# The last quarter of an MLP's second product in a seven-product form, and its LayerNorm on three engines

## The chip, the cores and the metric

The kernel runs on one core of a Trainium2 chip. A core has five engines that run side by side, each through its own queue in order: TensorE (PE) multiplies matrices into PSUM, VectorE (DVE), ScalarE (ACT) and GpSimd (POOL) work elementwise, and SyncE (SP) issues DMAs; ScalarE and GpSimd issue DMAs too. The metric is the time of one execution in microseconds on the device.

## What is computed

A decoder layer for 512 tokens of width 1024: LayerNorm, a token mixer, LayerNorm, an MLP with squared ReLU and hidden width 4096, LayerNorm. What this change touches is the end:

```python
h = layer_norm(DEEPNORM_ALPHA * h + mix, ln1_g[l], ln1_b[l])
ff = jnp.square(jax.nn.relu(h @ w_ff1[l])) @ w_ff2[l]
h = layer_norm(DEEPNORM_ALPHA * h + ff, ln2_g[l], ln2_b[l])
```

All is float32. Each float32 operand is split into a high part (rounded to a reduced float32) and a low part, the rest, and a product of two operands is three matmuls: high by high, high by low, low by high. The split of a weight tile is a copy on ScalarE (`hi`) and a subtraction on VectorE (`lo`), lines 180 and 181.

## The kernel before

**Stages.** The token mixer ends in line 1016; from there on the kernel works on `h1T`, the normalised tokens with channels on the partitions, and on `res`, four tiles of 128 tokens x 1024, which already hold alpha times the normalised tokens and to which the MLP is added. The hidden width is worked through in four quarters (`FC = 4`, line 323, loop in line 1135). A quarter has 1024 hidden channels in eight tiles of 128. Its first product (`gemm_fm`, line 221) makes the hidden tiles in blocks of 2 or 4 (`F1`, line 324); `ev_h` (line 1142) evicts them from PSUM with a ReLU and squares them.

**The second product, quarters one to three** (`win_f2`, line 1100). It is a scheme of Strassen's kind (Winograd's variant), seven products of half-sized blocks for eight. The 512 tokens are halved (token tiles 0, 1 and 2, 3), the output columns are halved (j = 0 and 1, 512 each), and the hidden tiles are taken in pairs. `win_sums` (line 1064) makes sums of weight blocks (T1, T2, T3; T4 in line 1122), `win_hid` (line 1082) sums of hidden blocks. `WIN` (line 327) lists the products: a name for the weight block, which half of the hidden pairs (`hf`), and a phase `ph` from 0 to 6. An entry is 2 pairs x 2 token tiles x 3 = 12 matmuls with 512 columns; 14 entries make 168 matmuls. Phases 0, 3 and 6 add onto one pair of PSUM banks, 2 and 5 onto another, 1 and 4 have their own. After the second half of a phase the bank, as it stands, is copied to an SBUF tile `ev` by ScalarE (line 1128) and added to one or two blocks of `res` by accumulating DMAs from GpSimd's queue (line 1130). A bank that is added to further can be written again only when its copy is done.

**The second product, last quarter** (line 1177 on). It is the plain form: `gemm_tm` (line 246) for token tiles 0 and 1, then 2, and then tile 3 written out, its last 512 columns in two halves of 256 (line 1185). VectorE adds the result from PSUM to `res` (`ev_res`, line 991).

**LN2** (`ln2`, line 1038) for a token tile: statistics and their aggregate on VectorE, a power of -0.5 on GpSimd (line 1047), then for each column half two passes on VectorE, subtract the mean and multiply by g (line 1050), multiply by the reciprocal deviation and add b (line 1051), and a DMA to the output. g and b are loaded to all partitions by `bcast_row` (line 98).

**What sets the order.** Weights come through one list `stream`; `pump` (line 157) issues the loads on SP two entries ahead and the splits one or two ahead. In quarters one to three the weights of the second product are loaded whole by `win_load` (line 1055) on GpSimd's queue, eight tiles of 512 KB, for the next quarter after the tenth entry (line 1131). `HOMES` (line 325) says into which buffers an entry's split goes: `w` has two of each, `r` uses the three buffers of the raw weights, `a` a pool of 24. Small work is spread between matmuls as generators (`spawn`, `tick`, `finish`, lines 196 to 216). The pool B has 22 buffers (line 58); `h1T` holds 16 of them until the last first product, a22 (line 1094) one per hidden pair until phase 4, and `relu` and `ev` use the rest. On top of this the framework plans the order of each engine's instructions and the buffers with a timeline of its own (`schedule_with_timeline_sim`, line 1243): an instruction whose operands or buffer are ready by that timeline can go ahead of one written earlier. On the chip each engine then keeps the planned order. `tc.issue_after` adds an instruction's place behind another on the same engine.

Of the kernel before, what the change touches and what calls it, by code (L numbers as in the profile page):

```python
# [10 lines left out]
F32 = mybir.dt.float32  # L11
# [41 lines left out]
def tile_hybrid_block(ctx: ExitStack, tc: tile.TileContext, I, out, dbg=None):  # L53
# [267 lines left out]


    FC = 4
    F1 = [((0, 4), (4, 2), (6, 2))] + [tuple((b, 2) for b in range(0, 8, 2))] * 2 + [((0, 4), (4, 4))]
    HOMES = "wwrawarawawawa"
    HOME = {"w": ("whi", "wlo"), "r": ("wraw", "wraw"), "a": ("xh", "xl")}
    WIN = (("11", 0, 0), ("21", 0, 1), ("11", 1, 0), ("21", 1, 1), ("T1", 0, 2), ("T1", 1, 2), ("T2", 0, 3), ("T2", 1, 3),
           ("T4", 0, 4), ("T4", 1, 4), ("22", 0, 5), ("22", 1, 5), ("T3", 0, 6), ("T3", 1, 6))
    fb = 0
    for ci in range(FC):  # L330
        nb = 8
        for b, w in F1[ci]:
            PL["f1", ci, b] = plan("w_ff1", (fb + b) * P, w * P, res=(ci == 0 and b == 0), per=8 // w)
        if ci < FC - 1:
            PL["f2", ci] = []
            for n, (op, hf, _) in enumerate(WIN):
                PL["f2", ci].append(len(stream))
                stream.append({"src": lambda q=(ci, op, hf): WQ[q], "nk": 2, "n": T, "res": False,
                               "ahead": 2, "home": HOMES[n]})
        else:  # L340
            plan_zip("f2last", [("w_ff2", 0, fb, True), ("w_ff2", T, fb, True)])
        fb += nb


# [693 lines left out]
    def ln2(tt, bst=None):  # L1038
        mv = S([P, 2], F32, "mv")
        r = res[tt]  # L1040
        if bst is None:
            bst = S([P, 2, 6], F32, "bst")
            for j in range(2):
                nc.vector.bn_stats(bst[:, j, :], r[:, j * T:(j + 1) * T])
        nc.vector.bn_aggr(mv, bst)
        vts(mv[:, 1:2], mv[:, 1:2], LN_EPS, None, op0=ALU.add)
        gtt(mv[:, 1:2], mv[:, 1:2], mhalf[:, 0:1], op=ALU.pow)
        for j in range(2):
            c = slice(j * T, (j + 1) * T)
            stt(r[:, c], r[:, c], mv[:, 0:1], bg[:, c], op0=ALU.subtract, op1=ALU.mult)  # L1050
            stt(r[:, c], r[:, c], mv[:, 1:2], bb[:, c], op0=ALU.mult, op1=ALU.add)
            nc.sync.dma_start(out[tt * P:(tt + 1) * P, c], r[:, c])
        yield

    def win_load(ci):
# [43 lines left out]

    def win_f2(ci, hid):  # L1100
        bank = {}
        for n, (op, hf, ph) in enumerate(WIN):
            i = PL["f2", ci][n]
            pump(i)
            hi, lo = stream[i]["w"]
            for pp in range(2):
                for t in range(2):
                    key = ({3: 0, 6: 0, 5: 2}.get(ph, ph), t)
                    opens = key not in bank
                    if opens:  # L1110
                        bank[key] = (PX if key[0] < 2 else MM)()
                    o, c = bank[key], slice(t * P, (t + 1) * P)
                    while ph not in hid[2 * hf + pp]:
                        tick(4)
                    xh, xl = hid[2 * hf + pp][ph]
                    mm(o, xh[:, c], hi[:, pp], start=opens, stop=False, skip_group_check=True)  # L1116
                    mm(o, xh[:, c], lo[:, pp], start=False, stop=False, skip_group_check=True)  # L1117
                    mm(o, xl[:, c], hi[:, pp], start=False, stop=hf == 1 and pp == 1, skip_group_check=True)  # L1118
                tick(4)
            if n in (5, 6):  # L1120
                t2, q21 = WT.pop((ci, n - 5))
                vtt(t2, t2, q21, op=ALU.subtract)
                WQ[ci, "T4", n - 5] = t2
            if hf == 1:
                for t in range(2):
                    o = bank[{3: 0, 6: 0, 5: 2}.get(ph, ph), t]
                    e = B([P, T], F32, "ev")
                    st["ev"] = act(e, o, AF.Copy, scale=-1.0 if ph == 4 else 1.0)  # L1128
                    for tt, j in (((0, 0),), ((0, 0),), ((2, 1),), ((0, 1),), ((2, 0),), ((0, 1),), ((2, 0), (2, 1)))[ph]:
                        nc.gpsimd.dma_start(res[tt + t][:, j * T:(j + 1) * T], e, accum_op=ALU.add)  # L1130
            if n == 9 and ci + 1 < FC - 1:
                win_load(ci + 1)

    WQ, WT = {}, {}
    for ci in range(FC):
        nb = 8
        hid = []
        win = ci < FC - 1
        if ci == 0:
            win_load(0)  # L1140

        def ev_h(a, ps):
            r = B([P, T], F32, "relu")
            act(r, ps, AF.Relu)  # L1144
            if win:
                if a % 2 == 0:
                    hid.append({"R": A([P, 2, T], F32, "hr")})
                ops = hid[-1]
                R = ops["R"]
                act(R[:, a % 2, :], r, AF.Square)  # L1150
                if a % 2:
                    h1 = A([P, 2, 2, 256], F32R, "h1p")
                    split(R[:, :, :256], h1[:, 0], h1[:, 1])
                    ops[0], ops[1] = [(h1[:, 0, i], h1[:, 1, i]) for i in range(2)]
                    spawn(win_hid(R, ops))
                return
            hh = A([P, 2, T], F32R, "hid0")
            act(hh[:, 0, :], r, AF.Square)
            gtt(r, r, r, op=ALU.mult)
            vtt(hh[:, 1, :], r, f(hh[:, 0, :]), op=ALU.subtract)  # L1160
            hid.append(hh)
        for b, w in F1[ci]:
            if ci == 0 and b == 0:
                gemm_fm(PL["f1", ci, b], h1T, T, ev_h, toks=slice(256, T), accs=accs)
                t_r1 = spawn(residual1())
            else:
                gemm_fm(PL["f1", ci, b], h1T, w * P, ev_h, width=2)
            if win and b == 0:
                t_ws = spawn(win_sums(ci))
        if ci == 0:  # L1170
            finish(t_r1)
        if win:
            finish(t_ws)
            for hf in range(2):
                WT[ci, hf] = (WQ[ci, "T2", hf], WQ[ci, "21", hf])
            win_f2(ci, hid)
        else:
            bg, bb = bcast_row("ln2_g"), bcast_row("ln2_b")
            gemm_tm(PL["f2last"], hid, T, ev_res, tts=(0, 1))
            spawn(ln2(0))  # L1180
            spawn(ln2(1))
            gemm_tm(PL["f2last"], hid, T, ev_res, tts=(2,))
            spawn(ln2(2))
            tt, r, bst = 3, res[3], S([P, 4, 6], F32, "bst4")
            for c0, n in ((0, T), (T, 256), (T + 256, 256)):
                acc = MM()[:, :n]
                ws = slice(c0 % T, c0 % T + n)
                for k in range(nb):
                    hi, lo = weights(PL["f2last"][c0 // T], k)
                    xh, xl = hid[k][:, 0, tt * P:], hid[k][:, 1, tt * P:]  # L1190
                    mm(acc, xh, hi[:, ws], start=k == 0, stop=False)
                    mm(acc, xh, lo[:, ws], start=False, stop=False)
                    mm(acc, xl, hi[:, ws], start=False, stop=k == nb - 1)
                    tick(None)
                vtt(r[:, c0:c0 + n], acc, r[:, c0:c0 + n], op=ALU.add)
                for j in range(c0 // 256, (c0 + n) // 256):
                    nc.vector.bn_stats(bst[:, j, :], r[:, j * 256:(j + 1) * 256])
            finish(spawn(ln2(3, bst)))


# [46 lines left out]
```

## Time and profile before

| | us |
|---|---|
| median of 3 runs (lowest, highest) | 903.61 (903.56, 903.88) |
| the profiled execution | 902.75 |
| its span, first to last instruction | 901.0 |
| MLP, first quarter's second product starts | 605.1 |
| second quarter's | 686.7 |
| last quarter's first MLP product ends, its second starts | 849.9 |

A profile row names the start and length in us, the engine, the source line and the operation, what is written <- what is read, and in brackets how long the engine sat idle before it and what it waited for. PE is the matmul, PEld the load of its stationary operand. A matmul's length contains its latency; two that follow each other start closer than that. Rows "xN" hold N instructions in a row.

### The profile page before, as it was taken

The page shows a single profiled execution, that of the slowest core. Times are in us where ns is not written, and L with a number is a line of the kernel's source. Part 1 is how long each engine was busy: PE and PEld are TensorE (multiplying, and loading weights), DVE is VectorE, ACT ScalarE, POOL GpSimd, SP SyncE. Part 2 cuts the span into 40 slices and gives each one's busy share as a digit, 9 for nine tenths or more (in the row PEclk, how much of TensorE's full clock was granted, in tenths as well). Part 3 has the DMA queues.
Part 4 walks back from the last instruction along what each step waited for, and adds up shares of the span by engine and source line. Part 5 has one row for each costly group of instructions (what it writes and reads, how often), then busy time and mean ns, then how long its engine had stood idle before and what let it go on. Part 6 is the DMA issues. An engine that isn't in the chain of part 4 may idle for free.

```text
span 901.0 us, 11740 instructions
## 1 busy us (share of the span) xinstructions
PE 883.8 (98%) x4508; PEld 751.3 (83%) x4508; DVE 553.4 (61%) x905; ACT 412.7 (46%) x701; POOL 170.1 (19%) x192
## 2 busy tenths in 40 slices
PE   6999999999999999999999999999999999999996
PEld 5988888888888888888888888988888888888886
DVE  7835855575635244657756797997557646723576
ACT  6455443444434333435645423366357546643410
POOL 1003442442511010000000002104400520141201
PEclk9999999999999999999999999999999999999999
DMA  7413313212212332212207618005950990494312
GB/s 244 121 47 94 91 51 94 71 47 71 76 38 92 88 105 70 72 41 66 94 24 258 210 47 303 2 0 138 301 121 25 265 247 25 107 213 104 126 69 83
DMA packets 61159, 97.80 MB, mean 109 GB/s; under 512 B 7552, under 2 KB 27392, under 8 KB 61104
## 3 DMA queue, kind: packets, MB, share of 16 engines
q1 hardware_dynamic: 48816, 68.23, 23.9%
q0 software_dynamic: 10368, 25.17, 11.6%
q10 hardware_dynamic: 1920, 3.66, 1.2%
q8 instruction: 35, 0.57, 0.3%
q14 instruction: 20, 0.16, 0.1%
HBM read 82.36 MB, written 2.10 MB: 94 GB/s over the span
## 4 chain that ended last, share of the span: by engine, by line
PE 97%; ACT 1%; POOL 1%; DVE 1%; DMA 1%; issue 0%; SPq 0%; DVEq 0%
PE mm L231 16%; PE mm L233 15%; PE mm L232 15%; PE mm L264 7%; PE mm L266 7%; PE mm L265 7%; PE px L1116 2%; PE px L1118 2%; PE px L1117 2%; PE mm L1116 2%; PE mm L1118 2%; PE mm L1117 2%; PE px L679 2%; PE px L836 1%; PE px L366 1%; PE px L264 1%
## 5 line engine op out<-in xcount | busy, mean ns | idle before, releaser
L181 DVE TENSOR_TENSOR wlo<-wraw,whi 128x1024 fp32r<-128x1024 f32 (+1 forms) x104 | 117.7, 1133 | 169.6 <-ACT whi L180 162.2
L231 PE MATMUL mm<-h,whi 128*128 128x512 f32 x416 | 162.6, 392 | 0.4 <-ACT gt L923 0.4
L232 PE MATMUL mm<-h,whi 128*128 128x512 f32 x416 | 162.3, 390 | 0.0
L180 ACT ACTIVATE whi<-wraw 128x1024 fp32r<-128x1024 f32 (+1 forms) x104 | 100.3, 964 | 134.1 <-PE mm L232 82.4
L233 PE MATMUL mm<-h,wlo 128*128 128x512 f32 x416 | 154.4, 390 | 0.0
L231 PEld LDWEIGHTS mm<-h,whi 128*128 128x128 f32 x416 | 78.1, 188 | 16.3 <-ACT gt L923 0.6
L233 PEld LDWEIGHTS mm<-h,wlo 128*128 128x128 f32 x416 | 77.9, 188 | 16.4 <-DVE wlo L181 0.3
L232 PEld LDWEIGHTS mm<-h,whi 128*128 128x128 f32 x416 | 78.1, 188 | 15.7
L1130 POOL DMA_DIRECT2D res<-ev x48 | 42.2, 1042 | 188.9 <-ACT ev L1128 151.5
L265 PE MATMUL mm<-wlo,h 128*128 128x512 f32 x128 | 50.3, 393 | 0.0
L266 PE MATMUL mm<-whi,h 128*128 128x512 f32 x128 | 50.1, 392 | 0.0
L264 PE MATMUL mm<-whi,h 128*128 128x512 f32 x128 | 49.7, 403 | 0.0
L351 POOL TENSOR_TENSOR mv<-mv,mhalf 128x1 f32<-128x1 f32 x4 | 4.6, 1155 | 211.5 <-DVE mv L350 211.5
L180 ACT ACTIVATE xh<-wraw 128x1024 fp32r<-128x1024 f32 (+1 forms) x28 | 27.3, 986 | 34.8 <-PE mm L266 16.1
L618 POOL TENSOR_TENSOR rp<-rp 128x256 f32<-128x256 f32 x32 | 31.5, 984 | 60.8 <-ACT E L623 44.0
L1144 ACT ACTIVATE relu<-mm 128x512 f32<-128x512 f32 x32 | 18.8, 596 | 50.7 <-PE mm L233 50.6
L625 DVE TENSOR_TENSOR M<-E,qk 128x512 f32<-128x512 f32 x32 | 27.3, 854 | 16.5 <-ACT E L623 16.5
L181 DVE TENSOR_TENSOR xl<-wraw,xh 128x1024 fp32r<-128x1024 f32 (+1 forms) x28 | 31.1, 1126 | 8.0 <-ACT xh L180 8.0
L623 ACT ACTIVATE E<-rp 128x512 f32<-128x512 f32 x32 | 20.4, 638 | 26.9 <-POOL rp L619 26.9
L619 POOL TENSOR_TENSOR rp<-rp 128x256 f32<-128x256 f32 x32 | 27.6, 862 | 10.3 <-ACT q L648 8.1
L266 PEld LDWEIGHTS mm<-whi,h 128*128 128x128 f32 x128 | 24.1, 188 | 5.0
L265 PEld LDWEIGHTS mm<-wlo,h 128*128 128x128 f32 x128 | 24.1, 188 | 4.3
(369 smaller groups left out, 2196.1 us busy)
## 6 DMA issues: line engine op xcount, KB each, us to landing
wraw<-in_w_in_dram SPq DMA_DIRECT2D x40, 512.0 KB, 3.5
wraw<-in_w_ff_dram SPq DMA_DIRECT2D x40, 512.0 KB, 4.5
wq<-in_w_ff_dram POOLq DMA_DIRECT2D x24, 512.0 KB, 8.8
res<-ev POOLq DMA_DIRECT2D x48, 256.0 KB, 6.6
wraw<-in_w_o_gla_dram SPq DMA_DIRECT2D x8, 512.0 KB, 3.7
wraw<-in_w_o_mla_dram SPq DMA_DIRECT2D x8, 512.0 KB, 3.2
wraw<-in_w_out_dram SPq DMA_DIRECT2D x8, 512.0 KB, 4.0
wraw<-in_w_in_dram SPq DMA_DIRECT2D x8, 360.0 KB, 5.1
```

The source lines that it names most:

```text
L180: st["ins"] = act(hi[:, :nk, :n], raw[:, :nk, :n], AF.Copy)
L181: vtt(lo[:, :nk, :n], raw[:, :nk, :n], f(hi[:, :nk, :n]), op=ALU.subtract)
L231: mm(o, hi[:, c], xh, start=first, stop=False)
L232: mm(o, hi[:, c], xl, start=False, stop=False)
L233: mm(o, lo[:, c], xh, start=False, stop=last)
L264: mm(o, xh, hi[:, :n], start=opens, stop=False, skip_group_check=share)
L265: mm(o, xh, lo[:, :n], start=False, stop=False, skip_group_check=share)
L266: mm(o, xl, hi[:, :n], start=False, stop=last, skip_group_check=share)
L1116: mm(o, xh[:, c], hi[:, pp], start=opens, stop=False, skip_group_check=True)
L1117: mm(o, xh[:, c], lo[:, pp], start=False, stop=False, skip_group_check=True)
L1118: mm(o, xl[:, c], hi[:, pp], start=False, stop=hf == 1 and pp == 1, skip_group_check=True)
L1130: nc.gpsimd.dma_start(res[tt + t][:, j * T:(j + 1) * T], e, accum_op=ALU.add)
```

## The change

The last quarter's second product takes the seven-product form too. Its weights are loaded by `win_load` like those of the others, its hidden tiles go through the same sums and splits, and its first product uses blocks of two. In `WIN` the entries of the weight block 22 (phase 5) and of T4 (phase 4) change places, for all quarters.

In the last quarter the first eight entries run as in the others, with eight copies and eight accumulating DMAs. The last six are regrouped by token tile: 22 for tile 0, 22 for tile 1, then T3 and T4 for tile 2, then T3 and T4 for tile 3, the T4 of tile 3 in two halves of 256 columns. These are added to `res` (or subtracted) by VectorE straight from PSUM, without a copy and a DMA.

LN2 of tiles 0 to 2 goes over three engines: the normalisation in one pass on ScalarE, the multiplication by g on VectorE (tile 0 first half and tile 2 second half: on GpSimd), the addition of b on GpSimd. The second half of tile 2 is put behind the power of tile 3 in GpSimd's order. Tile 3 keeps its four passes on VectorE, the two that need no power first.

```diff
-    F1 = [((0, 4), (4, 2), (6, 2))] + [tuple((b, 2) for b in range(0, 8, 2))] * 2 + [((0, 4), (4, 4))]
+    F1 = [((0, 4), (4, 2), (6, 2))] + [tuple((b, 2) for b in range(0, 8, 2))] * 3
...
     WIN = (("11", 0, 0), ("21", 0, 1), ("11", 1, 0), ("21", 1, 1), ("T1", 0, 2), ("T1", 1, 2), ("T2", 0, 3), ("T2", 1, 3),
-           ("T4", 0, 4), ("T4", 1, 4), ("22", 0, 5), ("22", 1, 5), ("T3", 0, 6), ("T3", 1, 6))
+           ("22", 0, 5), ("22", 1, 5), ("T4", 0, 4), ("T4", 1, 4), ("T3", 0, 6), ("T3", 1, 6))
...
+                           "ahead": 2, "home": "r" if ci == FC - 1 and n == 12 else HOMES[n]})
...
-        gtt(mv[:, 1:2], mv[:, 1:2], mhalf[:, 0:1], op=ALU.pow)
+        rstd = gtt(mv[:, 1:2], mv[:, 1:2], mhalf[:, 0:1], op=ALU.pow)
+        if tt == 3:
+            st["pow3"] = rstd
+        else:
+            nmr = S([P, 1], F32, "nmr")
+            stt(nmr, mv[:, 0:1], -1.0, mv[:, 1:2], op0=ALU.mult, op1=ALU.mult)
         for j in range(2):
             c = slice(j * T, (j + 1) * T)
-            stt(r[:, c], r[:, c], mv[:, 0:1], bg[:, c], op0=ALU.subtract, op1=ALU.mult)
-            stt(r[:, c], r[:, c], mv[:, 1:2], bb[:, c], op0=ALU.mult, op1=ALU.add)
-            nc.sync.dma_start(out[tt * P:(tt + 1) * P, c], r[:, c])
+            if tt < 3:
+                act(r[:, c], r[:, c], AF.Identity, scale=mv[:, 1:2], bias=nmr)
+                with ExitStack() as gates:
+                    if (tt, j) == (2, 1):
+                        while "pow3" not in st:
+                            yield
+                        gates.enter_context(tc.issue_after(st["pow3"].ins))
+                    (gtt if (tt, j) in ((0, 0), (2, 1)) else vtt)(r[:, c], r[:, c], gb[0][:, c], op=ALU.mult)
+                    gtt(r[:, c], r[:, c], gb[1][:, c], op=ALU.add)
+                nc.sync.dma_start(out[tt * P:(tt + 1) * P, c], r[:, c])
+            else:
+                stt(r[:, c], r[:, c], mv[:, 0:1], gb[0][:, c], op0=ALU.subtract, op1=ALU.mult)
+        if tt == 3:
+            yield
+            for j in range(2):
+                c = slice(j * T, (j + 1) * T)
+                stt(r[:, c], r[:, c], mv[:, 1:2], gb[1][:, c], op0=ALU.mult, op1=ALU.add)
+                nc.sync.dma_start(out[tt * P:(tt + 1) * P, c], r[:, c])
...
+        for n, (op, hf, ph) in enumerate(WIN[:8] if end else WIN):
+            pump(PL["f2", ci][n])
...
+            if end and n == 6:
+                gb.extend([bcast_row("ln2_g"), bcast_row("ln2_b")])
...
-            if n == 9 and ci + 1 < FC - 1:
+            if n == 9 and not end:
                 win_load(ci + 1)
...
+        pump(PL["f2", ci][13])
...
+        for t in range(2):
+            o = tile_product((8, 9), t)
+            vtt(res[t][:, T:], res[t][:, T:], o, op=ALU.add)
+            spawn(ln2(t))
+        bst = S([P, 4, 6], F32, "bst4")
+        for t in range(2):
+            r = res[2 + t]
+            o = tile_product((12, 13), t)
+            for j in (1, 0):
+                vtt(r[:, j * T:(j + 1) * T], r[:, j * T:(j + 1) * T], o, op=ALU.add)
+            if t == 0:
+                o = tile_product((10, 11), t)
+                vtt(r[:, :T], r[:, :T], o, op=ALU.subtract)
+                t_ln2 = spawn(ln2(2))
+                continue
+            for j in range(2):
+                nc.vector.bn_stats(bst[:, 2 + j, :], r[:, T + j * 256:T + (j + 1) * 256])
+            for j in range(2):
+                c = slice(j * 256, (j + 1) * 256)
+                o = tile_product((10, 11), t, j * 256, 256, PX()[:, :256])
+                vtt(r[:, c], r[:, c], o, op=ALU.subtract)
+                nc.vector.bn_stats(bst[:, j, :], r[:, c])
+        finish(spawn(ln2(3, bst)), t_ln2)
```

`product` (new, inside `win_f2`) is the old body of the loop, the three matmuls of one hidden pair and token tile; `tile_product` calls it for two entries, that is 12 matmuls, of one token tile. The plain form of the last quarter, its `plan_zip` and the squarings on GpSimd (line 1159) go.

More of the change, by code (lines that the diff above doesn't have):

```diff
@@ L1137, in tile_hybrid_block @@
         hid = []
-        win = ci < FC - 1
         if ci == 0:
@@ L1171, in tile_hybrid_block @@
             finish(t_r1)
[L1172 to L1198, printed above, removed]
+        finish(t_ws)
+        for hf in range(2):
+            WT[ci, hf] = (WQ[ci, "T2", hf], WQ[ci, "21", hf])
+        win_f2(ci, hid)
 _FLAT = {
```

84 lines of the change are left out of this document (43 added, 41 removed).

## The prediction

> **What bounds the kernel now.** I read the page's busy times and its chain of waits first, then the list of whom TensorE waited for, and only then the stages.
>
> ```profile
> span 901.0 us, 11740 instructions
> ...
> PE 883.8 (98%) x4508; PEld 751.3 (83%) x4508; DVE 553.4 (61%) x905; ACT 412.7 (46%) x701; POOL 170.1 (19%) x192
> ...
> PE 97%; ACT 1%; POOL 1%; DVE 1%; DMA 1%; issue 0%; SPq 0%; DVEq 0%
> ```
> ```profile
> PE px L366 <- ACT x L355: 8.8, 1, 8.8
> PE mm L233 <- DVE wlo L181: 0.5, 1, 0.5
> ```
> TensorE (PE) is the chain: 97% of it. Its only long wait, 8.8 us, is at the start; the next is half a microsecond. So a matmul taken away is time gained, one for one, as long as everything that feeds TensorE keeps up, and the last engine to finish after it does not get later. The prediction is therefore matmuls removed, minus waits that the new order makes, minus what the tail gets longer.
>
> **The matmuls removed.** The end of the program, matmul by matmul:
>
> ```profile
> 849.92 0.39 PE L264 MATMUL mm<-xh,hid 128*128 128x512 f32 x1
> ...
> 882.56 0.39 PE L1191 MATMUL mm<-xh,hid 128*128 128x512 f32 x1
> ...
> 888.00 0.28 PE L1191 MATMUL mm<-xh,hid 128*128 128x256 f32 x1
> ...
> 893.63 0.28 PE L1193 MATMUL mm<-xh,hid 128*128 128x256 f32 x1
> ```
> ```profile
> L264 PE MATMUL mm<-xh,hid 128*128 128x512 f32 x48 | 17.5, 389 | 0.0
> ...
> L1191 PE MATMUL mm<-xh,hid 128*128 128x256 f32 x16 | 4.5, 283 | 0.0
> ```
> The 0.39 is latency; the spacing counts. From 882.56 to 888.00 run 8 x 3 = 24 matmuls 512 wide: 0.2267 us each. From 888.00 to 893.63 lie 47 gaps of 256-wide ones: 0.1198 us each. The plain last product is 3 x 48 + 24 = 168 wide and 3 x 16 = 48 narrow ones: 168 x 0.2267 + 48 x 0.1198 = 43.8 us, which is what lies between 849.92 and the end. The seven-product form has 14 entries x 2 x 2 x 3 = 168 of them, of which the last 12 are cut into 24 narrow ones: 156 x 0.2267 + 24 x 0.1198 = 38.2 us. **Gain 5.6 us.** The first MLP product of that quarter keeps its 192 matmuls; only its blocks become narrower, as in the quarters before.
>
> **What feeds them.** The last quarter takes over the work of the others on the other engines: six weight sums and two more, 14 splits instead of 8, the sums and splits of the hidden tiles, 8 loads on the POOL queue instead of 8 on SP's, 8 evictions with 8 accumulating DMAs; it loses 8 squarings on GpSimd. The second quarter shows the same mix:
>
> ```profile
> 680.00:720.00 40.00, 40.00 (x178) 33.14 (x177) 27.66 (x30) 23.80 (x32) 13.95 (x18) 1.00 0.54 159
> ```
> VectorE (the third pair) is 69% busy, ScalarE 60%, GpSimd 35%, and TensorE does not stop. I cost this at nothing. The cover is gone only if an in-order engine waits with a split behind it: the rivals. The load of the LN2 rows goes from the third quarter to the last; it has the length of the seven-product phase to land.
>
> **The tail.** What follows the last matmul today, VectorE and then GpSimd:
>
> ```profile
> 893.95 0.42 DVE L1195 TENSOR_TENSOR res<-mm,res 128x256 f32<-128x256 f32 x1 [1.99 <-PE mm L1193]
> 894.41 0.43 DVE L1197 BATCH_NORM_STATS2 bst<-res 128x6 f32<-128x256 f32 x1
> 894.87 0.26 DVE L1045 BATCH_NORM_AGGREGATE mv<-bst 128x2 f32<-128x24 f32 x1
> 895.16 0.15 DVE L1046 TENSOR_SCALAR mv<-mv 128x1 f32<-128x1 f32 x1
> 895.24 1.40 DVE L1050 SCALAR_TENSOR_TENSOR res<-res,mv,bc 128x512 f32<-128x512 f32 x2
> 896.56 1.41 DVE L1051 SCALAR_TENSOR_TENSOR res<-res,mv,bc 128x512 f32<-128x512 f32 x2
> ```
> ```profile
> 895.40 0.99 POOL L1047 TENSOR_TENSOR mv<-mv,mhalf 128x1 f32<-128x1 f32 x1 [9.26 <-DVE mv L1046]
> ```
> The first two of the four passes over tile 3 already run beside the power on GpSimd, so writing them in that order gains nothing. Let M be the end of the last matmul, 893.91 (893.63 + 0.28). The power ends at M + 2.5, the last pass at M + 4.06, the span at M + 7.1. In the changed kernel tile 2's last half is held until the power of tile 3 is issued and then needs a multiply and an add on GpSimd. What these cost beside a working VectorE is shown by the squarings that the change removes:
>
> ```profile
> L1159 POOL TENSOR_TENSOR relu<-relu x8: 1037/1263/1725, 828.2 to 854.6; 128x512 f32<-128x512 f32 x8
> ...
> L1160 DVE TENSOR_TENSOR hid<-relu,hid x8: 678/1522/1526, 829.3 to 857.7; 128x512 fp32r<-128x512 f32 x8
> ```
> The columns are least, median and longest ns. Alone, GpSimd takes 1.04 us for 512 columns; with both at work VectorE's pass goes from 0.68 to 1.52. At 1.04 each, tile 2 ends at M + 2.5 + 2.1 = M + 4.6; at the longest, 1.73, at M + 6.0. The two last passes of tile 3, slowed to 1.52 each from M + 2.65, end at M + 5.7. Against M + 4.06 the tail is 0.5 to 1.9 us longer; both engines will be at work there, so I take the contended 5.7: **1.6 us lost.**
>
> The Trainium skill, on the page "SBUF — State Buffer" (section "SBUF: two separate sides"), says that VectorE operations with two SBUF inputs and GpSimd operations exclude each other by a lock held for a whole instruction. By that the two engines' work after the power would be done one after the other, 2 x 1.04 + 2 x 0.71 = 3.5 us, ending at M + 6.0 and the sum 0.3 us higher; the doubled median of L1160 agrees with it.
>
> **Before the tail** stands VectorE's queue. In the new form tiles 0 and 1 get their last product from PSUM by VectorE, on top of an accumulating DMA of the product before.
>
> ```profile
> res<-ev POOLq DMA_DIRECT2D x16, 256.0 KB, 4.7
> ```
> ```profile
> DMA to landing us min/median/max: 3.3/6.6/14.5
> ```
> ```profile
> 871.73 0.67 DVE L992 TENSOR_TENSOR res<-mm,res 128x512 f32<-128x512 f32 x1
> 872.32 0.68 DVE L1044 BATCH_NORM_STATS2 bst<-res 128x6 f32<-128x512 f32 x1
> 872.92 0.67 DVE L992 TENSOR_TENSOR res<-mm,res 128x512 f32<-128x512 f32 x1
> ```
> The first row is of the DMA view for 775 to 812 (median us from issue to landing), the second of all 48. The eighth entry ends at 849.92 + 96 x 0.2267 = 871.7; an eviction of 0.6 us and a landing of 4.7 put the first add at about 877.1, though its matmuls are done at 874.4. The last matmul ends near 888.3, so VectorE has 11.2 us. What can't be earlier: 7 adds of 0.67 and one of 0.42, 4 statistics of 0.68 and 3 of 0.43, three sets of small ones (0.26 + 0.15 + 0.15 each, an estimate from the rows of the tail), 4 multiplies of 0.67: 13.5 us by durations, and since back-to-back instructions start 0.60 apart (871.73 to 872.92 for two), about 12.0. That is 0.8 late with the landing of 4.7, nothing with 3.3 (12.6 us to work in), and 4.2 late if each of the four multiplies meets GpSimd and takes 0.84 more. I take **0.5 us lost**; before, VectorE idled 2 us ahead of the last matmul.
>
> **The sum.** The profiled execution took 902.75 (span 901.0 and 1.75 around it): 902.75 - 5.6 + 1.6 + 0.5 = 899.25. The median shown is 903.61, 0.86 above it: forecast **900.1** on that scale, with 898.0 if the tail costs nothing and 901.8 if it costs 3.8.
>
> **The rivals** come from the swap of the 22 and T4 entries, which holds for all quarters. Before, T4 stood between the eviction of T1's bank and the 22 product that adds onto it; now 22 comes one pair (5.4 us) sooner. And the four a22 tiles, which T4 reads, are held two entries longer, in a pool of 22 buffers of which h1T has 16: until T4, evictions have two buffers in turn, and each waits for a DMA.
>
> ```profile
> 627.56 0.60 ACT L1128 ACTIVATE ev<-mm 128x512 f32<-128x512 f32 x1 [2.40 <-DMA res<-ev]
> 629.13 0.60 ACT L1128 ACTIVATE ev<-mm 128x512 f32<-128x512 f32 x1 [0.97 <-DMA res<-ev]
> ...
> 706.94 0.60 ACT L1128 ACTIVATE ev<-mm 128x512 f32<-128x512 f32 x1 [1.52 <-DMA res<-ev]
> ...
> 722.61 0.60 ACT L1128 ACTIVATE ev<-mm 128x512 f32<-128x512 f32 x1 [4.70 <-DMA res<-ev]
> 724.14 0.60 ACT L1128 ACTIVATE ev<-mm 128x512 f32<-128x512 f32 x1 [0.94 <-DMA res<-ev]
> ```
> ```profile
> 627.56 0.39 PE L1116 MATMUL mm<-whi,a 128*128 128x512 f32 x1
> ```
> ```profile
> 709.16 0.39 PE L1116 MATMUL mm<-whi,a 128*128 128x512 f32 x1
> ```
> ```profile
> 719.36 0.39 PE L1116 MATMUL px<-whi,xh 128*128 128x512 f32 x1
> ...
> 720.04 0.39 PE L1116 MATMUL px<-whi,xh 128*128 128x512 f32 x1
> ```
> ```profile
> 703.81 5.31 POOL L1061 DMA_DIRECT2D wq<-in_w_ff_dram  x7
> 708.94 2.06 POOL L1130 DMA_DIRECT2D res<-ev  x2
> ```
> *A, a short stall at 22.* 627.56 and 709.16 are T4's second token tile in the first and second quarter; 22 takes these places. In the first the bank is evicted at 629.13 + 0.60 = 629.73: TensorE would stop 2.2 us. In the second it is evicted at 707.54, 1.6 us in time. The third becomes like the second, as it now loads for a next one. Against: the order on each engine is planned, and may put T4 first where 22 would wait. 900.1 + 2.2 = **902.3**.
>
> *B, slower: T3 waits for the evictions of T2.* These took a22 buffers before; without them they wait for the DMAs of T1's evictions, which stand behind seven weight loads in the POOL queue (703.81, then 708.94) and land only when the evictions at 722.61 and 724.14 are let go. T3 adds onto their bank from 719.36 and 720.04. It would stop until 722.61 + 0.60 = 723.2 (3.85 us), its second tile until 724.74 instead of 723.89 (0.85): 4.7 us in a quarter. It decides against the change from two quarters on, 900.1 + 9.4 = **909.5** (914.2 with three; one gives 904.8, no change). Against it: T4 runs in the 5.4 us ahead of T3, so its first a22 buffer comes free, after a quarter of it, 4 us before T3 starts, and a planner that sees the DMA late takes that one.
>
> *C, the full backlog.* Every multiply meets GpSimd, VectorE is 4.2 late instead of 0.5: **903.8**. For it: L1160's median is the contended one. Against: the adds read PSUM, and ScalarE takes over half of the passes.
>
> *D, no cost behind the last matmul* and passes of tiles 0 to 2 all done in time: 898.0 or a little below.
>
> **How the numbers follow.** Forecast (898.0 to 901.8) 0.55; A 0.15; C 0.10; B 0.13; D 0.07. A measurement here tells about 0.2% from no change, which is 1.8 us: faster is below 901.8, slower above 905.4. Faster: forecast, D and a part of A (0.03), 0.65. Same: the rest of A and C, 0.22. Slower: B, 0.13. The range goes from 898.0 over A and C to 905.5, where B with one quarter still lies; it leaves out D's lower part and B proper.
>
> **What would show it.** The gain: 36 matmul instructions fewer than 4,508 (156 + 24 for 168 + 48), and the last one ending 5.6 us sooner, near 888.3, if nothing stopped. A and B: rows in the list of TensorE's waits with ScalarE's ev as releaser, on L1116's successors, in the first three quarters, and the last quarter's start later than 849.9. The tail: the distance from the last matmul to the span's end, 7.1 now, 9.2 by my sum; GpSimd's two passes after the last power ending last. C: VectorE with no idle time ahead of the last add. The forecast is wrong if the last quarter starts more than 1 us late, or the distance is below 7.6 or above 11.

## The result, and the profile after

| | before | after |
|---|---|---|
| median of 6 runs each, us (lowest, highest) | 903.59 (902.65, 903.88) | 907.04 (905.80, 909.31) |
| the profiled execution, us | 902.75 | 906.14 |
| its span, us | 901.0 | 904.4 |
| last quarter's second product starts | 849.92 | 852.78 |
| last matmul starts | 893.63 | 890.92 |
| from the end of the last matmul to the end of the span | 7.1 | 13.2 |

The changed kernel is slower: 1.0042 times the time before (95% interval 1.0028 to 1.0057). The forecast was 900.1 with a range up to 905.5. The matmuls went, and more than they gave came back elsewhere.

The page of the changed kernel; the counts behind the x are instructions:

```profile
span 904.4 us, 11734 instructions
...
PE 878.9 (97%) x4472; PEld 746.3 (83%) x4472; DVE 571.9 (63%) x934; ACT 432.8 (48%) x733; POOL 180.8 (20%) x208
```

4,472 matmuls stand for 4,508, 36 fewer as forecast, and PE is busy 4.9 us less. The start of the last product (852.78) and the last matmul:

```profile
852.78 0.62 PE L1134 MATMUL px<-whi,h1p 128*128 128x512 f32 x2
```
```profile
890.92 0.28 PE L1136 MATMUL px<-xh,a 128*128 128x256 f32 x1
```

That is 38.14 us between the starts, against 43.71 before: 5.57 us gained, for 5.6 in the sum. But the product starts 2.86 us later. Whom PE waited for, over the whole span (us in total, times, longest):

```profile
PE px L363 <- ACT x L352: 9.2, 1, 9.2
PE px L1135 <- DVE wlo L181: 1.6, 1, 1.6
PE mm L233 <- DVE wlo L181: 0.5, 1, 0.5
PE mm L231 <- ACT gt L920: 0.4, 1, 0.4
```

The first wait, at the start of the program, was 8.8 before; the third and the fourth were there before with the same 0.5 and 0.4. With a new one of 0.2 further down the list, the waits account for 0.6 of the 0.94 us by which the MLP starts later (576.04 for 575.10). No line ahead of the MLP is changed. In the profiles of the kernels below, which share those lines, the first wait goes from 8.5 to 9.7 and the first quarter's second product starts anywhere from 604.9 to 607.0 (605.1 before, 606.1 after). So I take this as no effect of the change; no run shows it apart. The second row is new. It stands in the first quarter, whose second product takes 39.75 us in place of 37.85. All engines around it, in order of time:

```profile
629.13 0.60 ACT L1155 ACTIVATE ev<-mm 128x512 f32<-128x512 f32 x1 [5.01 <-DMA res<-ev]
...
630.03 0.85 POOL L1157 DMA_DIRECT2D res<-ev  x1 [4.77 <-ACT ev L1155]
...
630.60 6.04 POOL L1078 DMA_DIRECT2D wq<-in_w_ff_dram  x8
...
638.49 1.23 DVE L1086 TENSOR_TENSOR T<-wq,wq 128x1024 f32<-128x1024 f32 x1 [5.41 <-DMA wq<-in_w_ff_dram]
...
639.63 1.22 DVE L181 TENSOR_TENSOR wlo<-wq,whi 128x1024 fp32r<-128x1024 f32 x1
...
640.90 0.50 PE L1135 MATMUL px<-wlo,xh 128*128 128x512 f32 x1 [1.58 <-DVE wlo L181]
```

Read it downward: an eviction waits 5.0 us for a buffer that an accumulating DMA still reads. The DMA of this eviction is issued at 630.03, and the weight loads for the second quarter stand behind it in the same queue (630.60). VectorE, in order, waits 5.4 us for the first of them to sum weights of the next quarter, and behind that sum stands the low part of T3's weights, which PE needs now. Before, the first seven loads were issued 6.5 us sooner:

```profile
624.13 5.33 POOL L1061 DMA_DIRECT2D wq<-in_w_ff_dram  x7
```

The other loss is behind PE. VectorE's row of the first add of the last products, and the four multiplies by g with LN2's last rows:

```profile
880.10 0.69 DVE L1174 TENSOR_TENSOR res<-res,mm 128x512 f32<-128x512 f32 x1 [4.53 <-DMA res<-ev]
...
884.45 1.19 DVE L1059 TENSOR_TENSOR res<-res,bc 128x512 f32<-128x512 f32 x1
...
890.37 0.68 DVE L1059 TENSOR_TENSOR res<-res,bc 128x512 f32<-128x512 f32 x1
...
891.70 1.25 DVE L1059 TENSOR_TENSOR res<-res,bc 128x512 f32<-128x512 f32 x1
892.87 0.74 DVE L1192 TENSOR_TENSOR res<-res,px 128x256 f32<-128x256 f32 x2
893.53 1.30 DVE L1059 TENSOR_TENSOR res<-res,bc 128x512 f32<-128x512 f32 x1
```

And all engines from there to the last output:

```profile
895.83 0.15 DVE L1043 TENSOR_SCALAR mv<-mv 128x1 f32<-128x1 f32 x1
895.90 1.49 DVE L1063 SCALAR_TENSOR_TENSOR res<-res,mv,bc 128x512 f32<-128x512 f32 x2
896.14 1.00 POOL L1044 TENSOR_TENSOR mv<-mv,mhalf 128x1 f32<-128x1 f32 x1
...
897.11 1.40 POOL L1059 TENSOR_TENSOR res<-res,bc 128x512 f32<-128x512 f32 x1
897.31 3.41 DVE L1068 SCALAR_TENSOR_TENSOR res<-res,mv,bc 128x512 f32<-128x512 f32 x2
898.59 1.59 POOL L1060 TENSOR_TENSOR res<-res,bc 128x512 f32<-128x512 f32 x1
899.09 2.00 SPq L1069 DMA_DIRECT2D out_dram<-res  x2
901.18 0.39 SPq L1061 DMA_DIRECT2D out_dram<-res  x1
```

With M = 891.20, the end of the last matmul, the last statistic stands at M + 4.6 where it stood at M + 1.25: VectorE is 3.4 us late. The last two passes then take 3.41 us where they took 1.41, and the last output is issued behind the others on SP, at 901.18 though GpSimd was done at 900.18. From the last statistic to the end of the span it is 8.57 us, 5.84 before: 2.7 more. The whole difference of the spans: 0.9 (ahead of the MLP) + 1.9 (first quarter) - 5.6 + 3.4 + 2.7 = 3.3, for 3.4 measured.

### The profile page after: what moved, and what is told of

Same layout as the page of the kernel before. It is cut to its first block, busy times and chain, and to the rows that moved or that the text cites. A ratio compares the mean times of both kernels' runs of the same rounds, so it can differ in the third digit from the quotient of the medians.

```text
span 904.4 us, 11734 instructions
## 1 busy us (share of the span) xinstructions
PE 878.9 (97%) x4472; PEld 746.3 (83%) x4472; DVE 571.9 (63%) x934; ACT 432.8 (48%) x733; POOL 180.8 (20%) x208
## 3 DMA queue, kind: packets, MB, share of 16 engines
q0 software_dynamic: 12672, 31.46, 14.5%
## 5 line engine op out<-in xcount | busy, mean ns | idle before, releaser
L1157 POOL DMA_DIRECT2D res<-ev x56 | 48.4, 1014 | 243.5 <-ACT ev L1155 212.6
L620 ACT ACTIVATE E<-rp 128x512 f32<-128x512 f32 x32 | 20.4, 638 | 26.9 <-POOL rp L616 26.9
L180 ACT ACTIVATE xh<-wraw 128x1024 fp32r<-128x1024 f32 (+1 forms) x20 | 18.7, 952 | 24.8 <-PE mm L266 15.8
L1155 ACT ACTIVATE ev<-mm 128x512 f32<-128x512 f32 x20 | 11.9, 597 | 37.3 <-DMA res<-ev 26.7
L1086 DVE TENSOR_TENSOR T<-wq,wq 128x1024 f32<-128x1024 f32 x16 | 19.3, 1222 | 14.7 <-DMA wq<-in_w_ff_dram 14.5
```

Of the source, the lines that this page charges most:

```text
L180: st["ins"] = act(hi[:, :nk, :n], raw[:, :nk, :n], AF.Copy)
```

## The experiments

Medians and ratios are against runs of the kernel before on the same chip; "tail" is the distance from the end of the last matmul to the end of the span. The first kernel is the one before with an edit; all others are the changed kernel with the edits shown. Where a text names the old order, or T2 added from PSUM, these two edits are shown once, with the kernels of that name. The start of the last product and the tail are those of one profiled execution each.

| kernel | median, us | ratio (95%) | last product starts | tail |
|---|---|---|---|---|
| after | 907.04 | 1.0042 (1.0028 to 1.0057) | 852.78 | 13.2 |
| swap alone | 906.21 | 1.0037 (1.0023 to 1.0050) | 854.49 | 7.1 |
| first three as before | 903.73 | 1.0007 (0.9998 to 1.0016) | 850.42 | 13.2 |
| two more buffers | 904.82 | 1.0016 (1.0008 to 1.0025) | 852.23 | 12.6 |
| loads on SP | 909.69 | 1.0077 (1.0065 to 1.0089) | 858.46 | 13.4 |
| LN2 on VectorE | 905.35 | 1.0028 (1.0018 to 1.0039) | 852.19 | 12.2 |
| T2 added from PSUM | 905.95 | 1.0032 (1.0019 to 1.0044) | 853.87 | 12.6 |
| no GpSimd after the power | 900.92 | 0.9974 (0.9965 to 0.9984) | 850.47 | 10.4 |
| no multiplies | 900.05 | 0.9965 (0.9953 to 0.9978) | 849.86 | 9.9 |
| two tiles on GpSimd | 901.80 | 0.9984 (0.9975 to 0.9993) | 850.24 | 11.2 |
| ready first | 902.92 | 0.9998 (0.9989 to 1.0007) | 850.09 | 12.6 |
| no meeting | 903.84 | 1.0004 (0.9995 to 1.0013) | 850.68 | 13.1 |
| all on VectorE | 901.56 | 0.9984 (0.9975 to 0.9993) | 850.33 | 11.1 |

### Where the late start comes from

**The swap alone**: the kernel before, with only the entries exchanged.

```diff
-           ("T4", 0, 4), ("T4", 1, 4), ("22", 0, 5), ("22", 1, 5), ("T3", 0, 6), ("T3", 1, 6))
+           ("22", 0, 5), ("22", 1, 5), ("T4", 0, 4), ("T4", 1, 4), ("T3", 0, 6), ("T3", 1, 6))
```

> The kernel before with 22 and T4 exchanged in WIN and nothing else. Theory: the exchange itself makes TensorE wait in the first quarter, because T1's evictions have only two buffers, GpSimd's queue stands behind them, the next quarter's weights land late, and VectorE waits for them with T3's split behind it. It was 1.9 us in the changed kernel: 905.5 here (903.6 + 1.9), with one wait on the subtraction of line 181 near 640. Rival: the exchange costs nothing by itself, and the wait comes from other shifts in the order: 903.6 and no such wait.

903.23 before, 906.21 after the swap: it costs 3.0 us by itself. PE's waits from the first quarter on:

```profile
PE px L1117 <- DVE wlo L181: 1.5, 1, 1.5
PE mm L1116 <- ACT ev L1128: 0.9, 1, 0.9
```

The first is the stall of T3 seen above, at 641.2. The second, in the second quarter, is what rival A described: 22 waits for the eviction of T1's bank. The first quarter's second product takes 39.70 us and the second's 39.06, for 37.85 each. The second stall shows in this profile and in those of "T2 added from PSUM" (0.6 us) and "loads on SP" (1.4), not in the profiled execution of the changed kernel; what decides that is open.

**The first three as before**: the old order in quarters one to three, the new one in the last.

```diff
+    WIN0 = WIN[:8] + WIN[10:12] + WIN[8:10] + WIN[12:]
...
-        for n, (op, hf, ph) in enumerate(WIN[:8] if end else WIN):
+        for n, (op, hf, ph) in enumerate(WIN[:8] if end else WIN0):
```

> The changed kernel with the old order of 22 and T4 in the first three quarters; only the last quarter has the new one. Theory: the 1.9 us of the first quarter come back and nothing else: 905.1 (907.0 - 1.9). Rival: the wait has another cause and stays: 907.0.

All three quarters are back at the old times, and 3.3 us come back in the median (907.04 to 903.73), 1.4 more than the 1.9 that the first quarter lost in the profile of after. Between the two profiled executions it is 2.3 (906.14 to 903.80). The tail stays 13.2. So the swap explains nearly all of the loss against before, and without it 5.6 us of matmuls still buy nothing.

**Two more buffers** (pool B 24 for 22, another pool one less) and, in another kernel, **the loads on SP** instead of GpSimd's queue:

```diff
-    pb = ctx.enter_context(tc.tile_pool(name="pb", bufs=22))
+    pb = ctx.enter_context(tc.tile_pool(name="pb", bufs=24))
```
```diff
-                nc.gpsimd.dma_start(t, w2[:, k0:k0 + 3:2, j * T:(j + 1) * T])
+                (nc.gpsimd if ci == 0 else nc.sync).dma_start(t, w2[:, k0:k0 + 3:2, j * T:(j + 1) * T])
```

> The changed kernel with 24 buffers instead of 22 in the pool of the evictions, paid for with one of the 24 bigger ones of the weights' pool. After the run with the loads on SP, where the loads went out 7 us sooner and the wait became longer, the theory is this: what makes TensorE wait in the first quarter is that evictions have two buffers and wait in ScalarE's order for an accumulating DMA to land, with T3's split behind them. With four buffers T1's evictions need not wait, T3's split is in time, and 1.9 to 3.2 us are gone: 903.8 to 905.1. Rival: the evictions wait for the DMAs' order on GpSimd and not for buffers, or the weights' pool is as tight: 907.0 or more.

> The changed kernel, where the weights that a quarter loads for the next one are issued on SP's queue instead of GpSimd's; the order on VectorE stays but for one pair. Theory: the first quarter's wait comes about because those loads stand behind an accumulating DMA that waits for its eviction; on SP they go out earlier, VectorE's sums of the next quarter don't wait, T3's split is in time, and the 1.9 to 3.2 us of that quarter are gone: 903.8 to 905.1, with no wait of TensorE on line 181 near 640. Rival: the loads land as late there (the DMA engines are what is full), or the evictions alone make the wait: 907.0.

The first came as expected, the second missed. With two buffers more, the waits of evictions for accumulating DMAs between 600 and 660 us fall. The changed kernel's row, and the row of the two buffers:

```profile
ACT ev L1155 <- DMA res<-ev: 14.9, 7, 5.0
```
```profile
ACT ev L1155 <- DMA res<-ev: 3.2, 1, 3.2
```

The first quarter's second product takes 38.26 us for 39.75, and the median falls by 2.2. The two kernels differ by one more thing, the buffer taken from the other pool; its effect was not tried apart. With the loads on SP the theory of a queue that is merely in the wrong order fell. ScalarE's evictions in that kernel, and its loads (median us from issue to landing in the last column):

```profile
628.41 0.60 ACT L1155 ACTIVATE ev<-mm 128x512 f32<-128x512 f32 x1 [5.28 <-DMA res<-ev]
...
632.05 0.60 ACT L1155 ACTIVATE ev<-mm 128x512 f32<-128x512 f32 x1 [2.10 <-DMA res<-ev]
```
```profile
wq<-in_w_ff_dram SPq DMA_DIRECT2D x8, 512.0 KB, 12.7
```

The loads leave at 622.97 and no longer wait for an eviction, but they take 12.7 us each (7.3 in the same stretch of the changed kernel), the accumulating DMAs are no faster, the evictions wait again, and PE stops in more places: 909.69. At T3 it now waits for ScalarE, whose split stands behind the evictions:

```profile
640.35 0.86 PE L1134 MATMUL px<-whi,xh 128*128 128x512 f32 x2 [1.90 <-ACT whi L180]
```

So the wait of the evictions reaches PE by the loads or by the split, and more buffers take it away where moving the loads does not. But the wait alone does not stop PE. In the kernel before, the same row reads nearly as in the changed one, and PE runs through:

```profile
ACT ev L1128 <- DMA res<-ev: 13.7, 8, 4.7
```

What the swap changed is what the planned order puts behind the wait; that it came out so is seen in the rows, not tried apart.

### Where the tail comes from

**LN2 on VectorE**: the changed kernel with the four passes of before for every tile. **T2 added from PSUM**: in the last quarter VectorE adds the product of T2 to its one block, so that the first add of the last products waits for no DMA.

```diff
+                    if end and ph == 3:
+                        vtt(res[t][:, T:], res[t][:, T:], o, op=ALU.add)
+                        continue
```

> The changed kernel with LN2 as before, four passes on VectorE for every tile and GpSimd for the power alone. Theory: VectorE's queue sets the end, so 12 passes of 0.66 us in place of four multiplies (4.4 us in all) lengthen it by 3.5 us, and the last passes, which no longer meet GpSimd, get 2.6 us shorter: 907.9. Rival: sharing LN2 is what lengthened the tail; without GpSimd beside it VectorE is done sooner: 904.4.

> The changed kernel, where in the last quarter VectorE adds the T2 product of token tiles 0 and 1 from PSUM to res itself, without the copy and the accumulating DMA. Theory: VectorE's 4.5 us of waiting for that DMA goes, it begins tile 0 when its matmuls are done, 2.6 us sooner, and the backlog behind the last matmul shrinks by as much: 904.4. Rival: the backlog is the amount of work and its meeting with GpSimd, two adds more make it no smaller: 907.0.

Both missed. Taking the sharing of LN2 away was to cost, and the median came out 1.7 us lower; taking the DMA wait away, 1.1 lower. The intervals of both overlap with the changed kernel's, so the profiles have to say more. VectorE's last statistic, in the first and in the second, where M is the end of each kernel's own last matmul (890.60 and 892.29):

```profile
897.08 0.15 DVE L1043 TENSOR_SCALAR mv<-mv 128x1 f32<-128x1 f32 x1
```
```profile
896.37 0.15 DVE L1043 TENSOR_SCALAR mv<-mv 128x1 f32<-128x1 f32 x1
```

Without sharing it stands at M + 6.5, 1.9 later than in the changed kernel where 3.5 was expected, and the end follows 5.7 us behind it, 2.9 sooner. Without the DMA wait it stands at M + 4.1, only 0.5 sooner. Neither of them alone is the tail, so the next two leave work out on top of the old order in the first quarters. **No GpSimd after the power** leaves out the multiply by g and the addition of b for tile 2's second half. **No multiplies** adds T2 from PSUM and leaves out three of VectorE's four multiplies by g: tile 1's two and that of tile 2's first half.

```diff
-                    (gtt if (tt, j) in ((0, 0), (2, 1)) else vtt)(r[:, c], r[:, c], gb[0][:, c], op=ALU.mult)
-                    gtt(r[:, c], r[:, c], gb[1][:, c], op=ALU.add)
+                    if (tt, j) != (2, 1):
+                        (gtt if (tt, j) == (0, 0) else vtt)(r[:, c], r[:, c], gb[0][:, c], op=ALU.mult)
+                        gtt(r[:, c], r[:, c], gb[1][:, c], op=ALU.add)
```
```diff
-                    (gtt if (tt, j) in ((0, 0), (2, 1)) else vtt)(r[:, c], r[:, c], gb[0][:, c], op=ALU.mult)
+                    if (tt, j) in ((0, 0), (2, 1)):
+                        gtt(r[:, c], r[:, c], gb[0][:, c], op=ALU.mult)
+                    elif tt == 0:
+                        vtt(r[:, c], r[:, c], gb[0][:, c], op=ALU.mult)
```

> The kernel of the run with the old order in the first three quarters, without the two GpSimd passes over the second half of tile 2 after the last power; that half leaves out the multiplication by g and the addition of b. Theory: these passes double VectorE's last two (3.41 us instead of 1.41) and their output goes last: the tail gets 2.6 us shorter, 13.2 to 10.6, time 901.1 (903.7 - 2.6). Rival: VectorE's last passes are slow for another reason: tail 13.2, 903.7.

> The old order in the first three quarters, the T2 product added from PSUM, and VectorE's three multiplications by g for tile 1 and the first half of tile 2 left out (that output lacks g). Theory: with the wait for the DMA gone, these multiplies, which stand among the last adds and statistics and meet GpSimd, are the rest of the backlog: the last statistics come 2.8 us sooner than in the run with the adds from PSUM, tail 12.6 to 9.8, time 900.3. Rival: the backlog is made ahead of them, by the power of tile 1 standing behind GpSimd's adds: no more than 0.6 us gained, 902.5 or later.

Both came as expected. In the first, VectorE's last two passes take their old time with nothing on GpSimd beside them:

```profile
893.48 0.15 DVE L1044 TENSOR_SCALAR mv<-mv 128x1 f32<-128x1 f32 x1
893.55 1.49 DVE L1065 SCALAR_TENSOR_TENSOR res<-res,mv,bc 128x512 f32<-128x512 f32 x2
894.96 1.40 DVE L1070 SCALAR_TENSOR_TENSOR res<-res,mv,bc 128x512 f32<-128x512 f32 x2
```

From the last statistic to the end it is 5.8 us again (893.48 to 899.3); the backlog ahead of it is untouched, the statistic stands at M + 4.6. In the second it is the other way round:

```profile
889.73 0.15 DVE L1044 TENSOR_SCALAR mv<-mv 128x1 f32<-128x1 f32 x1
889.80 1.40 DVE L1067 SCALAR_TENSOR_TENSOR res<-res,mv,bc 128x512 f32<-128x512 f32 x2
891.12 3.42 DVE L1072 SCALAR_TENSOR_TENSOR res<-res,mv,bc 128x512 f32<-128x512 f32 x2
```

The statistic stands at M + 1.5 and the passes take 3.42. The two losses are separate: 2.7 us behind the power from GpSimd's two passes, 3.1 us ahead of it from VectorE's queue, in which the multiplies and the wait for the DMA stand. By "T2 added from PSUM" the wait is 0.5 of these, which leaves some 2.6 for the three multiplies.

### Is there a division of LN2 that keeps the gain?

Four kernels, all with the old order in the first three quarters and T2 added from PSUM. **Two tiles on GpSimd**: tiles 0 and 1 by ScalarE and GpSimd alone, tiles 2 and 3 by four passes on VectorE. **Ready first**: tile 0 on VectorE, tile 1 on ScalarE and GpSimd, tile 2 on three engines. **No meeting**: as that, with the small product for ScalarE's bias on GpSimd, and each half of tile 2 multiplied and added to on one engine. **All on VectorE**: the twelve passes of tiles 0 to 2 that the changed kernel had shared out go back.

```diff
+        if tt < 2:
...
+                gtt(r[:, c], r[:, c], gb[0][:, c], op=ALU.mult)
+                gtt(r[:, c], r[:, c], gb[1][:, c], op=ALU.add)
```
```diff
+        if tt in (1, 2):
...
+                (gtt if tt == 1 else vtt)(r[:, c], r[:, c], gb[0][:, c], op=ALU.mult)
+                gtt(r[:, c], r[:, c], gb[1][:, c], op=ALU.add)
```
```diff
+            gtt(nmr, nmr, mv[:, 1:2], op=ALU.mult)
...
+                e = vtt if (tt, j) == (2, 1) else gtt
+                e(r[:, c], r[:, c], gb[0][:, c], op=ALU.mult)
+                e(r[:, c], r[:, c], gb[1][:, c], op=ALU.add)
```
```diff
+            stt(r[:, c], r[:, c], mv[:, 0:1], gb[0][:, c], op0=ALU.subtract, op1=ALU.mult)
+            stt(r[:, c], r[:, c], mv[:, 1:2], gb[1][:, c], op0=ALU.mult, op1=ALU.add)
```

> A version to beat both: the old order in the first three quarters, the T2 product added from PSUM, tiles 0 and 1 normalised on ScalarE and multiplied and added on GpSimd alone, tiles 2 and 3 in four passes on VectorE as in the kernel before. Theory: VectorE has no multiplies in the stretch of the last matmuls, GpSimd is done with its passes before the last power, so the backlog is about 1 us and the last passes take 1.41: tail 8.5 instead of 13.2, 899.0. Rival: GpSimd's eight passes of 1.3 us are late and hold the powers of tiles 2 and 3: tail 11 to 12, 901.5 to 902.5.

> A second version to beat both: the old order in the first three quarters, the T2 product added from PSUM; tile 0 in four passes on VectorE, tile 1 on ScalarE and GpSimd, tile 2 on ScalarE, VectorE (g) and GpSimd (b), tile 3 as before. In the planned order only tile 2's two multiplies stand behind tile 3's statistics. Theory: the statistics of tile 3 end about 1 us after the last matmul as in the kernel before, so the backlog is gone; GpSimd's two adds of tile 2 meet VectorE's last passes and cost 2: tail 10, 900.5. Rival: VectorE is still behind by the work of tile 0, tail 11.3 as in the version before, 901.8.

> A third version: like the second, but minus mean times deviation is made by GpSimd right behind the power, the first half of tile 2 is multiplied and added on GpSimd, the second half on VectorE. Theory: half as many passes lie behind VectorE's last statistics as in the second version, but GpSimd's two of tile 2 come after the last power, so the last passes still meet them: tail 10 to 10.5, 900.5 to 901.0. Rival: tile 2's normalisation no longer waits in VectorE's order, its GpSimd passes are done before tile 3's last ones, tail 9, 899.5.

> The seven-product last quarter alone: the old order of 22 and T4 in the first three quarters, the product of tile 2's first halves (tokens tile 0 and 1, last products) as changed, the product of T2 added by VectorE straight from PSUM instead of by eviction and accumulating DMA, and LN2 of all four tiles by the four passes on VectorE of the kernel before, none on ScalarE or GpSimd. Theory (the shared LN2 costs more than it takes from VectorE, and the wait for the accumulating DMA is the other part of the backlog): the tail of the run with LN2 on VectorE was 12.2; with that wait gone it loses the 2.7 us between its last statistics and those of the runs without the wait, tail 9.5, last matmul near 888.3 as in the runs with the old order, 900.0 to 900.4, below every kernel that shares LN2. Rival (VectorE has simply too much to do in the last 16 us, twelve passes of 0.71 being about as much as the multiplies and their meetings with GpSimd): VectorE stays about 5 us behind, tail 10.9 to 11.3 as with tiles 0 and 1 shared, 901.3 to 901.8.

In the first and the last the time was the rival's, and the two between missed. The rival of "two tiles on GpSimd" had GpSimd late for two powers; it was late for tile 2's (ready at 886.07, begun at 888.47), but for tile 3's it waited 2.4 us for VectorE. VectorE there has four passes fewer of LN2 for each of two tiles than with all on VectorE, and is no earlier:

```profile
876.31 0.69 DVE L1166 TENSOR_TENSOR res<-res,mm 128x512 f32<-128x512 f32 x1 [1.75 <-PE mm L1125]
...
883.56 0.77 DVE L1048 SCALAR_TENSOR_TENSOR nmr<-mv 128x1 f32<-128x1 f32 x1
...
886.00 3.06 DVE L1056 SCALAR_TENSOR_TENSOR res<-res,mv,bc 128x512 f32<-128x512 f32 x2
...
895.53 1.41 DVE L1057 SCALAR_TENSOR_TENSOR res<-res,mv,bc 128x512 f32<-128x512 f32 x2
```

From its first add to its last pass VectorE needs 20.6 us (876.31 to 896.94), as in the changed kernel (880.10 to 900.72). Its two passes beside GpSimd take 3.06 for 1.41. In "ready first" one instruction on a single column shows the same meeting:

```profile
889.21 2.48 POOL L1054 TENSOR_TENSOR res<-res,bc 128x512 f32<-128x512 f32 x2
889.22 1.27 DVE L1048 SCALAR_TENSOR_TENSOR nmr<-mv 128x1 f32<-128x1 f32 x1
```

1.27 us, for 0.15 elsewhere, and it stands ahead of tile 3's last statistic. The Trainium skill, on the page "SBUF — State Buffer" (section "Who interferes with whom"), has a VectorE instruction with two SBUF inputs and a GpSimd instruction that reads SBUF hold one port pair in turn, each for a whole instruction. The traces agree: this one-column product reads SBUF twice and waits out a whole pass of GpSimd. "No meeting" moved it to GpSimd, and GpSimd became late:

```profile
890.55 0.15 DVE L1044 TENSOR_SCALAR mv<-mv 128x1 f32<-128x1 f32 x1
...
891.67 1.78 POOL L1057 TENSOR_TENSOR res<-res,bc 128x512 f32<-128x512 f32 x1
893.41 0.99 POOL L1048 TENSOR_TENSOR mv<-mv,mhalf 128x1 f32<-128x1 f32 x1
```

The power of tile 3 could start at 890.7 and stands behind an addition until 893.41. With all passes back on VectorE nothing meets, yet VectorE has no idle time either. Its first row, and then the busy times of PE, PEld, DVE, ACT and POOL from there to its end and to the end of the last matmul:

```profile
876.40 0.69 DVE L1158 TENSOR_TENSOR res<-res,mm 128x512 f32<-128x512 f32 x1 [2.07 <-PE mm L1117]
```
```profile
876.40:897.00 20.60, 12.34 (x65) 10.47 (x63) 20.26 (x41) 0.00 (x0) 3.69 (x4) 0.92 0.21 77
876.40:888.70 12.30, 12.30 (x65) 10.47 (x63) 12.20 (x23) 0.00 (x0) 1.85 (x2) 1.00 0.17 63
```

20.4 us from the first add to the end of the last pass at 896.80, of which only 12.3 lie beside matmuls. That is what the new form of the last quarter has done: the first of tiles 0 and 1 is not complete until 12 us before the end of the last matmul, where before VectorE had added all four blocks of both by 873.6, 20 us before it. VectorE then has all four tiles' LN2 ahead of it. "All on VectorE" and "two tiles on GpSimd" are faster than the kernel before by 0.16% (interval 0.07% to 0.25%), and their difference of 0.2 us is not resolved. The old order together with more buffers was not tried.

## Why the prediction was wrong

- **The matmuls removed, 5.6 us**: right, 5.57.
- **What feeds them, "I cost this at nothing"**: wrong, by 1.9 us in the first quarter of the profile and by about 3 in the medians (3.0 for the swap alone, 3.3 when it is undone). The profile of the swap alone shows another 1.2 in the second quarter. The condition was named, an in-order engine that waits with a split behind it, and the cause too, the a22 tiles held longer in a pool of 22. The rivals then put the wait on PE itself, for an eviction: A at 22, B at T3. It came at T3 by another way, through a weight load delayed behind an eviction's DMA and VectorE's wait for that load. B had the loads ahead of the accumulating DMAs, as in the trace of before; the planned order turned that round. A's own stall appears in the second quarter in three of the profiles (0.6 to 1.4), and in the first only with the loads on SP (0.3).
- **Before the tail, "0.5 us lost"**: this is the term that failed by most in the changed kernel's own end. It measured 3.4. The first add came when forecast, 11.1 us before the last matmul's end (11.2 forecast). The work in that stretch was mis-sized: 12.0 us by back-to-back spacing, and 14.5 by the rows (880.10 to the statistic at 895.83, less the 1.25 that follow the last matmul in any case). Three of the four multiplies met GpSimd and took 1.19, 1.25 and 1.30, which makes 4.42 for the four in place of 2.4, and VectorE waited 0.74 for GpSimd's first power; the two make 2.8, for an excess of 2.5. Rival C had this mechanism with 4.2 us and a chance of 0.10. Its counter-argument, that ScalarE takes over half of the passes, does not hold: with all passes on VectorE its last stretch took 20.4 us, and with twelve of them shared out 20.6.
- **The tail, 1.6 us**: right in mechanism, 2.7 in size. After the power VectorE and GpSimd took 3.58 us together (897.14 to 900.72), where I had set 3.04, passes of 1.52 side by side. The rule of the Trainium skill that the prediction cites (page "SBUF — State Buffer", section "SBUF: two separate sides") has the two engines' passes one after the other, which was worked out as 3.5, and the trace agrees with that. The agreement is partly luck: with the 1.26 that a GpSimd pass with two different inputs takes when it waits for nothing (893.02 and 894.92 in the changed kernel), in place of the 1.04 of a squaring, the same sum is 3.9. The other 0.6 is the output issue, behind two others on SP.
- **The sum**: with the measured terms, 902.75 + 0.9 + 1.9 - 5.6 + 3.4 + 2.7 = 906.05, the profiled execution being 906.14. The range failed because it let one rival happen at a time. The stall of the swap (A and B, 0.15 and 0.13), C's backlog (0.10) and a tail longer than forecast came together, and the rivals had been weighed as if each excluded the others.

## What to carry to other kernels

When matmuls at the end of a kernel are regrouped, list for each other engine the work that only becomes ready in the last stretch, and compare it with the time left: here VectorE had 20 us of work to do from the moment the first of it became ready, 12 us before the end of the last matmul, and the 5.6 us of matmuls saved were mostly paid back there. Passes given to GpSimd saved VectorE nothing here where both read two operands from SBUF at the same time (20.6 us for 20.4); look for the meeting in the rows before counting the gain. An exchange in a list that all stages share has to be priced in each stage by who holds which buffer for how long, and rivals that rest on different resources are added and not weighed against each other.

## What the runs showed of the hardware that was not expected

An operation's width said little about what a meeting costs: the product on one column took 0.77 and 1.27 us beside GpSimd for 0.15 alone. VectorE's work that does not read SBUF twice was untouched: in the changed kernel, GpSimd adds from 885.16 for 2.88 us, and VectorE's two additions from PSUM beside it keep their spacing of 0.6.

```profile
885.62 1.27 DVE L1181 TENSOR_TENSOR res<-res,px 128x512 f32<-128x512 f32 x2
886.81 0.68 DVE L1041 BATCH_NORM_STATS2 bst<-res 128x6 f32<-128x512 f32 x1
```

Weight loads moved from GpSimd's queue to SP's were issued earlier and took longer to land, 12.7 us at the median for 7.3. The queue is not the whole of it: in the kernel before, GpSimd's loads issued from 624.13 on, nearly as early, took 9.7. What the queue itself does was not tried apart.
